# Sums of the upper tiles taken from turned blocks, eight transposes per tile, in the entries of a Strassen-like decoder block

## Chip, cores, metric

One Trainium2 core of one chip runs the whole kernel. The metric is the device time of one execution in microseconds (us). Before the change three runs gave 1890.28, 1890.79 and 1891.32 us; the median is 1890.79.

## The reference

The kernel computes one decoder block in fp32: two SwiGLU half-steps around a gated mixer. All of it is matrix products over 1024 rows of 1024 numbers, with a norm of the rows ahead of each part.

```python
def swiglu(x, w1, w3, w2):
    return (jax.nn.silu(x @ w1) * (x @ w3)) @ w2
...
        h = h + 0.5 * swiglu(rms_norm(h, ffn1_norm[l]), ffn1_w1[l], ffn1_w3[l], ffn1_w2[l])
...
    return rms_norm(h, final_norm)
```

Between the first half-step and a second one of the same form stands the mixer: its input is rms(h) times one combined weight (queries, keys, values, pooling, gates), and its output is added to h. What the change touches is how the left operand of three of these products, the normed rows X of the first half-step, of the mixer and of the second half-step, is turned and summed.

## The kernel before

**Sevens.** Each of these products is done in quarters: X is turned and cut into four blocks of 512 by 512, b11 and b21 from the first four tiles of 128 rows (their columns 0 to 511, `LOWS`, and 512 to 1023, `HIGHS`), b12 and b22 likewise from the last four. A product of 2 by 2 blocks takes seven block products in place of eight. `Quad.run` names them by number: 1 takes b11, 2 takes b21, 3 takes b22, 4 takes the sum t4, 5 takes t1, 6 takes t2 and 7 takes t3. Here t1 = b12 - b11, t2 = b22 - t1, t3 = b22 - b12 = t2 - b11 and t4 = t2 - b21. The turned b11 and b21 are kept in SBUF as `low`. The weights have sums of their own: s1 (L370), s2 (L374), s3 (L378), s4 (L383), made in `Quad.summed`.

**Two parts.** Every fp32 operand is split in a rounded part (hi, written by ScalarE) and a lower part (lo = value - hi, by VectorE or GpSimd). For weights that is `Sevens.split` (L320 ScalarE, L323 VectorE or GpSimd), for X it is `Rows` (transposes L409, hi L411, lo L416) and `Parts` (hi L429, lo L432). A product is three groups of four matmuls (L332): hi by hi, lo by hi, hi by lo.

**Entries.** `Entry.run` treats tiles 4 to 7 (the upper tiles). It runs three times: in the first half-step (some 36 to 65 us in the profile), in the mixer (654 to 682) and in the second half-step (1249 to 1278). For each tile it does two products whose operands are ready (`self.product(i)`, `self.product(k)`: numbers 1 and 2 on several column blocks of weights), and between them the next tile's rows are normed (`high(t, 1)`, the row scaling of L282 on VectorE, whose 1/rms is a power on GpSimd, L279) and turned. `self.operand(n)` makes the two parts of the weight for a later product on ScalarE and GpSimd, `self.out(n)` takes a finished product's bank on, `self.more(...)` makes operands of the first products behind the entry: `more(0, 2)` makes s2 on GpSimd, `more(0)` splits it for product 6, `more(1)` makes and splits s3 for product 7. Behind the last tile come products 6, 7, 5 and 4 (t2, t3, t1, t4).

**What sets the order.** Each engine executes its instructions in the order in which the code writes them (a manual schedule); semaphores make one engine wait for another. A wait at the head of an engine's list holds all behind it. The banks of PSUM named "acc" and "mm" are given out in turn.

Before, a tile has 12 transposes: 4 of b22 (`Rows`), 4 of b12 (`turned`, L477) and 4 of the row difference (`HIGHS` less `LOWS`) that GpSimd makes ahead of them (L461) and that gives t3 turned. VectorE makes t1 in place in the bank of b12 (L471), t2 by adding b11 to the turned t3 (L465), t4 in place of t2 (L468), and all the lower parts of X.

Of the kernel before, what the change touches and what calls it, by code (L numbers as in the profile page):

```python
# [10 lines left out]
F32 = mybir.dt.float32  # L11
F32R = mybir.dt.float32r
AF = mybir.ActivationFunctionType
OP = mybir.AluOpType
# [5 lines left out]
NT = S // P  # L20
# [117 lines left out]
def tile_block(  # L138
# [29 lines left out]
    ve, ac, gp, pe = nc.vector, nc.scalar, nc.gpsimd, nc.tensor  # L168
# [10 lines left out]
    def bank(tag, name):  # L179
        return psum.tile([P, HALF], F32, tag=tag, name=name)  # L180
# [18 lines left out]
    h = []  # L199
# [98 lines left out]
    LOWS, HIGHS = slice(0, HALF), slice(HALF, S)  # L298
# [7 lines left out]
    class Sevens:  # L306


        def __init__(self, name, X, fw, fs=None):
            self.name, self.X, self.fw, self.fs = name, X, fw, fs or fw  # L310
            self.n_lo = 0
            self.terms = (0, 1, 2)
            self.led = {}
# [86 lines left out]
    class Rows:  # L400
# [14 lines left out]
        def lower(self):  # L415
            ve.tensor_tensor(self.lo, self.p, self.hi.bitcast(F32), op=OP.subtract)  # L416
# [5 lines left out]
    class Parts:  # L422


        def __init__(self, X, what, src, t):
            q = t % 4
            self.hi, self.lo = (v[:, :, q * P:(q + 1) * P] for v in X[what])
            self.src = src.rearrange("p (k q) -> p k q", k=4)
            ac.activation(self.hi, self.src, AF.Copy)  # L429

        def lower(self):
            ve.tensor_tensor(self.lo, self.src, self.hi.bitcast(F32), op=OP.subtract)  # L432

    class Entry:

# [17 lines left out]
        def run(self, high, after, first=0):  # L453


            X = self.sv.X

            def scaled_rows(t):
                y = high(t, 1)
                t3 = self.sv.half_tile("s", f"t3_{t}")  # L460
                gp.tensor_tensor(t3, y[:, HIGHS], y[:, LOWS], op=OP.subtract)  # L461
                return y, t3

            def second(r3, t2, t):
                ve.tensor_tensor(t2, r3.flat, self.low[t - 4][:, LOWS], op=OP.add)  # L465

            def fourth(t2, t):
                ve.tensor_tensor(t2, t2, self.low[t - 4][:, HIGHS], op=OP.subtract)  # L468

            def first_less(p12, t):  # L470
                ve.tensor_tensor(p12, p12, self.low[t - 4][:, LOWS], op=OP.subtract)  # L471

            def turned(y, t):
                p12 = bank("acc", f"x_b12_{t}")
                for j in range(4):
                    c = slice(j * P, (j + 1) * P)
                    pe.transpose(p12[:, c], y[:, c], ident)  # L477
                return p12

            y, t3 = scaled_rows(4)  # L480
            for t in range(4, NT - 1):
                i = first + 2 * (t - 4)
                k = i + 1
                self.product(i)
                self.operand(i + 2)
                high(t + 1, 0)
                s = Rows(X, "b22", y[:, HIGHS], t)
                self.out(i)
                p12 = turned(y, t)
                first_less(p12, t)  # L490
                r1 = Parts(X, "t1", p12, t)
                r3 = Rows(X, "t3", t3, t)
                t2 = bank("acc", f"x_t2_{t}")
                s.lower()
                r1.lower()
                self.product(k)
                y, t3 = scaled_rows(t + 1)
                self.operand(k + 2)
                second(r3, t2, t)
                r2 = Parts(X, "t2", t2, t)  # L500
                r3.lower()
                r2.lower()
                self.out(k)
                after(t)
                fourth(t2, t)
                if t < NT - 2:
                    r4 = Parts(X, "t4", t2, t)
                    if t > 4:
                        self.more(0, 1)
                    r4.lower()  # L510

            t = NT - 1
            i, k = i + 2, k + 2
            self.product(i)
            p3 = bank("acc", f"x_t3_{t}")
            p12 = turned(y, t)
            s = Rows(X, "b22", y[:, HIGHS], t, "mm")
            r3 = Rows(X, "t3", t3, t, p=p3)
            r4 = Parts(X, "t4", t2, t - 1)
            self.more(0, 2)  # L520
            t2 = bank("acc", f"x_t2_{t}")
            second(r3, t2, t)
            r4.lower()
            r2 = Parts(X, "t2", t2, t)
            r3.lower()
            self.more(0)
            r2.lower()
            self.product(k)
            self.out(i)
            first_less(p12, t)  # L530
            r1 = Parts(X, "t1", p12, t)
            self.more(1)
            r1.lower()
            fourth(t2, t)
            r4 = Parts(X, "t4", t2, t)
            s.lower()
            r4.lower()
            self.out(k)
            after(t)


# [364 lines left out]
    X = sums_of_x(scope.enter_context(sbuf("x1")), "f1", SUMS)  # L906
# [1099 lines left out]
    first = first_w_o()  # L2006
    with tc.manual_schedule():
# [8 lines left out]
        for q in range(N // 2):  # L2016
# [20 lines left out]
            u, i = divmod(q, NT // 2)  # L2037
# [59 lines left out]
    op = wo.enter_context(sbuf("ops", "right"))  # L2097
# [390 lines left out]
```

## Time and profile before

| what | us |
|---|---|
| median of three runs | 1890.79 |
| span of the profiled execution | 1888.4 |
| TensorE busy (8806 matmuls) | 1878.1 |
| VectorE busy | 1345.8 |
| ScalarE busy | 773.1 |
| GpSimd busy | 715.0 |

The median stands 2.4 us above the span; the profiled execution's own time beyond its span is not known, and the 2.4 us are taken for what lies around it. TensorE is named PE, VectorE DVE, ScalarE ACT, GpSimd POOL. A row of the timeline gives the start from the span's beginning, the duration, the engine, the line, the operation, what is written and read, the count of like instructions in the row, and in brackets how long the engine had been idle and for what it waited. Names such as `x_t` and `x_b` are banks of PSUM (the turned sums and blocks of X), `xhi_t`, `xlo_t`, `xhi_b`, `xlo_b` the two parts of X's sums and blocks, `wc` the two parts of a weight, `s_` sums of weights or rows, `u_` the banks of the products, `nst` the norm's column. `f1`, `mix` and `f2` stand for the three entries.

### The profile page before, as it was taken

The numbers are of one execution on the slowest core, as the hardware profiler recorded it, in microseconds if no ns is written. First come the engines' busy times: TensorE is split into PE (matmuls) and PEld (weight loads), VectorE is DVE, ScalarE is ACT, GpSimd is POOL, SyncE is SP. The second block draws the span as 40 slices with busy tenths as digits, with TensorE's granted clock in tenths as the row PEclk, the third lists the DMA queues.
The fourth block names the chain that finished last, engine by engine and source line by source line (L and its number), as shares of the span: only waits on it lengthen the run. The fifth ranks groups of instructions, "written<-read, shape, count | busy, mean of one in ns | idle before, by whom it ended". The sixth has DMA issues, their size and how long they took to land.

```text
span 1888.4 us, 24712 instructions
## 1 busy us (share of the span) xinstructions
PE 1878.1 (99%) x8806; PEld 1559.8 (83%) x8806; DVE 1345.8 (71%) x1988; ACT 773.1 (41%) x1395; POOL 715.0 (38%) x536
## 2 busy tenths in 40 slices
PE   9999999999999999999999999999999999999998
PEld 8888888888888888888888888888888888888886
DVE  6877666558786776657885897887665566577867
ACT  7423333333344543334445772363233333334344
POOL 5433333331223354434555357543333333312221
PEclk9999999999999999999999999999999999999999
DMA  6154423336565526765578968644332223354654
GB/s 258 34 201 158 139 93 115 126 117 217 171 230 197 184 90 217 231 221 200 206 245 315 321 221 297 260 150 155 140 129 96 87 102 118 135 193 159 225 198 145
DMA packets 146035, 334.98 MB, mean 177 GB/s; under 512 B 17784, under 2 KB 39288, under 8 KB 144376
## 3 DMA queue, kind: packets, MB, share of 16 engines
q1 hardware_dynamic: 142168, 322.55, 49.4%
q10 hardware_dynamic: 3744, 10.85, 1.6%
q8 instruction: 69, 1.13, 0.2%
q14 instruction: 54, 0.44, 0.1%
HBM read 232.76 MB, written 100.60 MB: 177 GB/s over the span
## 4 chain that ended last, share of the span: by engine, by line
PE 54%; DVE 3%; ACT 2%; issue 1%; DMA 1%; POOL 0%; ACTq 0%; SPq 0%; DVEq 0%; POOLq 0%
PE u_mixm L332 15%; PE d_f L846 8%; PE wo L2168 4%; PE yp L1910 1%; PE u_f20b L332 1%; PE u_f21a L332 1%; PE u_f210b L332 1%; PE u_f210a L332 1%; PE u_f29b L332 1%; PE u_f29a L332 1%; PE u_f28b L332 1%; PE u_f28a L332 1%; PE u_f27b L332 1%; PE u_f27a L332 1%; PE u_f26b L332 1%; PE u_f25b L332 1%
## 5 line engine op out<-in xcount | busy, mean ns | idle before, releaser
L846 PE MATMUL d_f<-bhi_f,ahi_f 128*128 128x512 f32 x616 | 240.2, 390 | 0.0
L846 PE MATMUL d_f<-bhi_f,alo_f 128*128 128x512 f32 x616 | 239.7, 389 | 0.0
L846 PE MATMUL d_f<-blo_f,ahi_f 128*128 128x512 f32 x616 | 239.6, 389 | 0.0
L803 POOL TENSOR_TENSOR alo_f<-g_f,ahi_f 128x512 fp32r<-128x512 f32 x60 | 86.5, 1457 | 273.1 <-ACT ahi_f L799 273.1
L332 PE MATMUL u_mixm<-xhi_t_mix,wc_mixm 128*128 128x512 f32 x608 | 157.3, 391 | 0.2 <-ACT wc_mixm L320 0.2
L846 PEld LDWEIGHTS d_f<-bhi_f,ahi_f 128*128 128x128 f32 x616 | 115.6, 188 | 24.2 <-ACT h L420 0.4
L846 PEld LDWEIGHTS d_f<-bhi_f,alo_f 128*128 128x128 f32 x616 | 115.6, 188 | 24.1
L846 PEld LDWEIGHTS d_f<-blo_f,ahi_f 128*128 128x128 f32 x616 | 115.6, 188 | 23.9
L332 PEld LDWEIGHTS u_mixm<-xhi_t_mix,wc_mixm 128*128 128x128 f32 x608 | 113.5, 188 | 24.0 <-ACT wc_mixm L320 0.7
L332 PE MATMUL u_mixm<-xhi_b_mix,wc_mixm 128*128 128x512 f32 x456 | 120.3, 391 | 0.0
L323 POOL TENSOR_TENSOR wc_mixm<-s_mixm,wc_mixm 128x512 fp32r<-128x512 f32 x52 | 76.8, 1477 | 107.1 <-ACT wc_mixm L320 94.2
L332 PEld LDWEIGHTS u_mixm<-xhi_b_mix,wc_mixm 128*128 128x128 f32 x456 | 84.9, 188 | 17.3
L320 ACT ACTIVATE wc_mixm<-s_mixm 128x512 fp32r<-128x512 f32 x76 | 47.0, 628 | 111.8 <-DVE s_mixm L374 56.0
L799 ACT ACTIVATE ahi_f<-g_f 128x1024 fp32r<-128x1024 f32 x84 | 81.9, 975 | 4.9 <-DMA g_f<-gs_f 4.9
L332 PE MATMUL u_mixm<-xlo_t_mix,wc_mixm 128*128 128x512 f32 x304 | 81.3, 389 | 0.0
L323 POOL TENSOR_TENSOR wc_mixm<-raw,wc_mixm 128x512 fp32r<-128x512 f32 x40 | 60.2, 1505 | 40.2 <-ACT wc_mixm L320 29.5
L2168 PE MATMUL wo<-w_o,o_hi 128*128 128x512 f32 x224 | 69.4, 391 | 0.0
L799 ACT ACTIVATE bhi_f<-s_f2w 128x512 fp32r<-128x512 f32 x55 | 32.9, 628 | 86.3 <-DVE s_f2w L821 67.3
L799 ACT ACTIVATE bhi_f<-s_f1w 128x512 fp32r<-128x512 f32 x55 | 33.0, 629 | 83.6 <-DVE s_f1w L821 70.3
L332 PEld LDWEIGHTS u_mixm<-xlo_t_mix,wc_mixm 128*128 128x128 f32 x304 | 57.1, 188 | 12.0
L803 DVE TENSOR_TENSOR alo_f<-g_f,ahi_f 128x1024 fp32r<-128x1024 f32 (+1 forms) x48 | 57.6, 1200 | 9.4 <-ACT ahi_f L799 9.4
L332 PE MATMUL u_mixm<-xlo_b_mix,wc_mixm 128*128 128x512 f32 x228 | 61.0, 389 | 0.0
(1351 smaller groups left out, 4765.5 us busy)
## 6 DMA issues: line engine op xcount, KB each, us to landing
g_f<-gs_f SPq DMA_DIRECT2D x70, 512.0 KB
gs_f<-y_f SPq DMA_DIRECT2D x88, 256.0 KB
raw<-in_w2a_dram SPq DMA_DIRECT2D x35, 512.0 KB
raw<-in_w2b_dram SPq DMA_DIRECT2D x35, 512.0 KB
gs_f<-gb_f SPq DMA_DIRECT2D x46, 256.0 KB
raw<-in_w1a_dram SPq DMA_DIRECT2D x22, 512.0 KB
raw<-in_w3a_dram SPq DMA_DIRECT2D x22, 512.0 KB
raw<-in_w1b_dram SPq DMA_DIRECT2D x22, 512.0 KB
```

Source lines behind the costliest of these rows:

```text
L320: ac.activation(w[:, 0], src, AF.Copy)
L323: eng.tensor_tensor(w[:, 1], src, w[:, 0].bitcast(F32), op=OP.subtract)
L332: pe.matmul(p, a, b, start=(start and n == 0), stop=(n == 11), skip_group_check=not start)
L799: ac.activation(hi[:, c], src, AF.Copy)
L803: eng.tensor_tensor(lo[:, d], src[:, o], hi[:, d].bitcast(F32), op=OP.subtract)
L846: pe.matmul(self.banks[m][t], l, r, start=(first and q == 0), stop=(last and q == 2))
L1910: pe.matmul(p, a, b, start=(j == 0), stop=(j == 11))
L2168: pe.matmul(banks[m][t], l, r, start=(st == 0 and j == 0 and q == 0), stop=(st == 1 and j == 1 and q == 2))
```

## The change

Of each upper tile only b22 and b12 are turned: 8 transposes. The row difference on GpSimd and its 4 transposes go. t1 = b12 - b11 is written to the lower half of the tile's own rows in SBUF (`h[t][:, LOWS]`), t2 = b22 - t1 goes into a bank, t3 = t2 - b11 over the bank of b12, t4 = t2 - b21 to the upper half of the tile's own rows. `Parts` gets a `higher()` that may be issued later, and a `lower(eng)`. In tiles 4 to 6 the lower parts of t1 and t4 are made by GpSimd, t4's hi and lo one tile later. The operand of product i + 2 is now asked for ahead of its tile as `operand(i + 4)` at the end of the tile before. In tile 7 the order of sums, parts, `more` and `out` is another.

```diff
-        def __init__(self, X, what, src, t):
+        def __init__(self, X, what, src, t, now=True):
...
+            if now:
+                self.higher()
+
+        def higher(self):
             ac.activation(self.hi, self.src, AF.Copy)
 
-        def lower(self):
-            ve.tensor_tensor(self.lo, self.src, self.hi.bitcast(F32), op=OP.subtract)
+        def lower(self, eng=ve):
+            eng.tensor_tensor(self.lo, self.src, self.hi.bitcast(F32), op=OP.subtract)
...
             def scaled_rows(t):
-                y = high(t, 1)
-                t3 = self.sv.half_tile("s", f"t3_{t}")
-                gp.tensor_tensor(t3, y[:, HIGHS], y[:, LOWS], op=OP.subtract)
-                return y, t3
-
-            def second(r3, t2, t):
-                ve.tensor_tensor(t2, r3.flat, self.low[t - 4][:, LOWS], op=OP.add)
+                return high(t, 1)
+
+            def first_less(p12, t):
+                t1 = h[t][:, LOWS]
+                ve.tensor_tensor(t1, p12, self.low[t - 4][:, LOWS], op=OP.subtract)
+                return t1
+
+            def second(s, t1, t2):
+                ve.tensor_tensor(t2, s.flat, t1, op=OP.subtract)
+
+            def third(t2, p, t):
+                ve.tensor_tensor(p, t2, self.low[t - 4][:, LOWS], op=OP.subtract)
 
             def fourth(t2, t):
-                ve.tensor_tensor(t2, t2, self.low[t - 4][:, HIGHS], op=OP.subtract)
-
-            def first_less(p12, t):
-                ve.tensor_tensor(p12, p12, self.low[t - 4][:, LOWS], op=OP.subtract)
+                t4 = h[t][:, HIGHS]
+                ve.tensor_tensor(t4, t2, self.low[t - 4][:, HIGHS], op=OP.subtract)
+                return t4
...
+            def turned_rows(y, t, tag="acc"):
+                return Rows(X, "b22", y[:, HIGHS], t, tag)
+
+            y = scaled_rows(4)
+            self.operand(first + 2)
+            r4 = None
             for t in range(4, NT - 1):
                 i = first + 2 * (t - 4)
                 k = i + 1
                 self.product(i)
-                self.operand(i + 2)
                 high(t + 1, 0)
-                s = Rows(X, "b22", y[:, HIGHS], t)
+                s = turned_rows(y, t)
+                p12 = turned(y, t)
                 self.out(i)
-                p12 = turned(y, t)
-                first_less(p12, t)
-                r1 = Parts(X, "t1", p12, t)
-                r3 = Rows(X, "t3", t3, t)
+                if r4 is not None:
+                    r4.higher()
+                    r4.lower(gp)
+                t1 = first_less(p12, t)
                 t2 = bank("acc", f"x_t2_{t}")
                 s.lower()
-                r1.lower()
+                second(s, t1, t2)
                 self.product(k)
-                y, t3 = scaled_rows(t + 1)
+                y = scaled_rows(t + 1)
+                r2 = Parts(X, "t2", t2, t)
+                r1 = Parts(X, "t1", t1, t)
+                third(t2, p12, t)
+                r1.lower(gp)
                 self.operand(k + 2)
-                second(r3, t2, t)
-                r2 = Parts(X, "t2", t2, t)
-                r3.lower()
                 r2.lower()
                 self.out(k)
+                r3 = Parts(X, "t3", p12, t)
+                r3.lower()
+                r4 = Parts(X, "t4", fourth(t2, t), t, False)
                 after(t)
-                fourth(t2, t)
-                if t < NT - 2:
-                    r4 = Parts(X, "t4", t2, t)
-                    if t > 4:
-                        self.more(0, 1)
-                    r4.lower()
+                self.operand(i + 4)
+                if t > 4:
+                    self.more(0, 1)
 
             t = NT - 1
             i, k = i + 2, k + 2
             self.product(i)
-            p3 = bank("acc", f"x_t3_{t}")
             p12 = turned(y, t)
-            s = Rows(X, "b22", y[:, HIGHS], t, "mm")
-            r3 = Rows(X, "t3", t3, t, p=p3)
-            r4 = Parts(X, "t4", t2, t - 1)
+            s = turned_rows(y, t, "mm")
+            r4.higher()
+            r4.lower(gp)
+            t1 = first_less(p12, t)
+            t2 = bank("acc", f"x_t2_{t}")
+            second(s, t1, t2)
             self.more(0, 2)
-            t2 = bank("acc", f"x_t2_{t}")
-            second(r3, t2, t)
-            r4.lower()
             r2 = Parts(X, "t2", t2, t)
+            third(t2, p12, t)
+            self.more(0)
+            self.out(i)
+            r2.lower()
+            r3 = Parts(X, "t3", p12, t)
             r3.lower()
-            self.more(0)
-            r2.lower()
             self.product(k)
-            self.out(i)
-            first_less(p12, t)
-            r1 = Parts(X, "t1", p12, t)
+            r1 = Parts(X, "t1", t1, t)
+            r4 = Parts(X, "t4", fourth(t2, t), t, False)
             self.more(1)
             r1.lower()
-            fourth(t2, t)
-            r4 = Parts(X, "t4", t2, t)
+            r4.higher()
+            self.out(k)
             s.lower()
             r4.lower()
-            self.out(k)
             after(t)
```

What this does to the order on the engines is shown at the end of the mixer's entry. First GpSimd, from the weights of tile 6 to the first products behind the entry; `s_mixt` are the row differences, `xlo_t_mix<-h` lower parts of t1 and t4, L374 is s2. Before:

```order
L323 TENSOR_TENSOR wc_mixm_5662<-raw_5398,wc_mixm_5662 128x512
L323 TENSOR_TENSOR wc_mixm_5688<-raw_5336,wc_mixm_5688 128x512
L279 TENSOR_TENSOR nst_5602<-nst_5602,mhalf 128x1
L461 TENSOR_TENSOR s_mixt_7_5731<-hn_mix_5601 128x512
L323 TENSOR_TENSOR wc_mixm_5733<-raw_5398,wc_mixm_5733 128x512
L374 TENSOR_TENSOR s_mixm_5773<-s_mixm_5672,raw_5287 128x512
L323 TENSOR_TENSOR wc_mixm_5780<-s_mixm_5773,wc_mixm_5780 128x512
```

The same stretch of GpSimd after the change:

```order
L323 TENSOR_TENSOR wc_mixm_5625<-raw_5374,wc_mixm_5625 128x512
L323 TENSOR_TENSOR wc_mixm_5633<-raw_5312,wc_mixm_5633 128x512
L279 TENSOR_TENSOR nst_5571<-nst_5571,mhalf 128x1
L436 TENSOR_TENSOR xlo_t_mix<-h_3181,xhi_t_mix 128x4x128
L436 TENSOR_TENSOR xlo_t_mix<-h_3183,xhi_t_mix 128x4x128
L323 TENSOR_TENSOR wc_mixm_5690<-raw_5374,wc_mixm_5690 128x512
L436 TENSOR_TENSOR xlo_t_mix<-h_3183,xhi_t_mix 128x4x128
L374 TENSOR_TENSOR s_mixm_5727<-s_mixm_5636,raw_5263 128x512
L323 TENSOR_TENSOR wc_mixm_5731<-s_mixm_5727,wc_mixm_5731 128x512
```

The row difference is gone, two lower parts stand in its place, and a third (t4 of tile 6) stands ahead of s2.

Next ScalarE in tile 7 of the mixer's entry, from the rounding of b22 on; `xhi_t_mix<-x_t_7` and `x_b_7` are roundings of the sums in banks, `wc_mixm<-s_mixm` those of s2 and s3, `y_m` output copies. Before:

```order
L411 ACTIVATE xhi_b_mix<-x_b_7_5761 128x4x128
L411 ACTIVATE xhi_t_mix<-x_t_7_5755 128x4x128
L429 ACTIVATE xhi_t_mix<-x_t_6_5714 128x4x128
L429 ACTIVATE xhi_t_mix<-x_t_7_5775 128x4x128
L320 ACTIVATE wc_mixm_5780<-s_mixm_5773 128x512
L1233 ACTIVATE y_m_0_5699<-u_mixm_5675 128x512
L429 ACTIVATE xhi_t_mix<-x_b_7_5756 128x4x128
L320 ACTIVATE wc_mixm_5801<-s_mixm_5799 128x512
```

The same stretch of ScalarE after the change (`h_3183` holds t1 and t4 of tile 6, `h_3185` those of tile 7):

```order
L411 ACTIVATE xhi_b_mix<-x_b_7_5716 128x4x128
L433 ACTIVATE xhi_t_mix<-h_3183 128x4x128
L433 ACTIVATE xhi_t_mix<-x_t_7_5725 128x4x128
L320 ACTIVATE wc_mixm_5731<-s_mixm_5727 128x512
L1247 ACTIVATE y_m_0_5664<-u_mixm_5638 128x512
L433 ACTIVATE xhi_t_mix<-x_b_7_5711 128x4x128
L433 ACTIVATE xhi_t_mix<-h_3185 128x4x128
L320 ACTIVATE wc_mixm_5754<-s_mixm_5752 128x512
```

The rounding of t3, second in the list before, now stands behind the rounding of s2 and an output copy; t4 of tile 6 stands directly behind b22.

Last VectorE in the same tile, from the sums to s3 (L378). Before:

```order
L465 TENSOR_TENSOR x_t_7_5775<-x_t_7_5755,h_3201 128x512
L432 TENSOR_TENSOR xlo_t_mix<-x_t_6_5714,xhi_t_mix 128x4x128
L416 TENSOR_TENSOR xlo_t_mix<-x_t_7_5755,xhi_t_mix 128x4x128
L432 TENSOR_TENSOR xlo_t_mix<-x_t_7_5775,xhi_t_mix 128x4x128
L471 TENSOR_TENSOR x_b_7_5756<-x_b_7_5756,h_3201 128x512
L378 TENSOR_TENSOR s_mixm_5799<-raw_5287,raw_5401 128x512
```

The same stretch of VectorE after the change:

```order
L467 TENSOR_TENSOR h_3185<-x_b_7_5711,h_3177 128x512
L471 TENSOR_TENSOR x_t_7_5725<-x_b_7_5716,h_3185 128x512
L474 TENSOR_TENSOR x_b_7_5711<-x_t_7_5725,h_3177 128x512
L436 TENSOR_TENSOR xlo_t_mix<-x_t_7_5725,xhi_t_mix 128x4x128
L436 TENSOR_TENSOR xlo_t_mix<-x_b_7_5711,xhi_t_mix 128x4x128
L478 TENSOR_TENSOR h_3185<-x_t_7_5725,h_3177 128x512
L378 TENSOR_TENSOR s_mixm_5752<-raw_5263,raw_5377 128x512
```

The lower part of t3 (the second L436), which waits for t3's rounding on ScalarE, and the fourth sum (L478) now stand ahead of s3.

More of the change, by code (lines that the diff above doesn't have):

```diff
@@ L478, in turned @@
                 return p12
-            y, t3 = scaled_rows(4)
+            def turned_rows(y, t, tag="acc"):
[3 more added lines that the diff above has]
+            r4 = None
             for t in range(4, NT - 1):
```

## The prediction

> **What bounds the kernel now.** First the busy shares on the page, then the waits of TensorE alone.
>
> ```profile
> span 1888.4 us, 24712 instructions
> PE 1878.1 (99%) x8806; PEld 1559.8 (83%) x8806; DVE 1345.8 (71%) x1988; ACT 773.1 (41%) x1395; POOL 715.0 (38%) x536
> PEclk9999999999999999999999999999999999999999
> ```
>
> ```profile
> PE idle L967 <- DVE mhalf L198: 1.1, 1, 1.1
> PE x_t L409 <- POOL s_f1t L461: 0.8, 1, 0.8
> PE o L1851 <- DVE elo L1833: 0.3, 1, 0.3
> ```
>
> TensorE works for 1878.1 of 1888.4 us at full granted clock, and its longest wait inside the work is 0.8 us, once, on the difference that GpSimd makes for the first entry. So time goes away only where TensorE gets less to do or that wait goes, and any new wait of TensorE is added to the span: nothing later has slack to take it back. The run's own time is the span plus 2.4 us (1890.79 against 1888.4); a measurement of this kernel tells about 0.2% (3.8 us) from no change.
>
> **What goes.** One whole upper tile of the mixer's entry on TensorE, then the first of the first entry:
>
> ```profile
> 661.05 0.60 PE L409 MATMUL x_b<-ident,hn_mix 128*128 128x128 f32 x4
> 661.49 0.60 PE L477 MATMUL x_b<-ident,hn_mix 128*128 128x128 f32 x4
> 661.92 0.60 PE L409 MATMUL x_t<-ident,s_mixt 128*128 128x128 f32 x4
> 662.28 1.17 PE L332 MATMUL u_mixm<-xhi_b_mix,wc_mixm 128*128 128x512 f32 x4
> ```
>
> ```profile
> 36.83 0.60 PE L477 MATMUL x_b<-ident,x 128*128 128x128 f32 x4
> 38.25 0.65 PE L409 MATMUL x_t<-ident,s_f1t 128*128 128x128 f32 x4 [0.82 <-POOL s_f1t L461]
> ```
>
> Groups of four transposes start 0.44 us apart, although each group's bar is 0.60 us long (they overlap); three groups take 662.28 - 661.05 = 1.23 us. I take 0.435 us for the group that goes. Four tiles in three entries give 12 x 0.435 = 5.2 us, and the 0.82 us wait goes with its writer: 6.0 us in all. The Trainium skill, "TensorE: Matmul & The Clock Gate", Part 4, gives about 275 ns for a transpose in one kernel's context; by that 48 of them would be worth an estimated 13.2 us. The rows disagree: the pitch decides, 0.109 us each.
>
> **What is late next.** In each entry the path leaves the transposes at the last tile (7), where the first products on the new sums begin. The rows of the mixer's entry, engine by engine; t2 names the product at 678.76, t3 the next, which starts 0.91 us into the 680.71 row (half of it), at 681.62.
>
> ```profile
> 674.66 0.60 PE L477 MATMUL x_b<-ident,hn_mix 128*128 128x128 f32 x4
> 675.10 0.60 PE L409 MATMUL x_b<-ident,hn_mix 128*128 128x128 f32 x4
> 678.76 1.19 PE L332 MATMUL u_mixm<-xhi_t_mix,wc_mixm 128*128 128x512 f32 x4
> 680.71 2.00 PE L332 MATMUL u_mixm<-xhi_t_mix,wc_mixm 128*128 128x512 f32 x8
> ```
>
> ```profile
> 674.46 1.27 POOL L323 TENSOR_TENSOR wc_mixm<-raw,wc_mixm 128x512 fp32r<-128x512 f32 x1
> 675.70 1.28 POOL L374 TENSOR_TENSOR s_mixm<-s_mixm,raw 128x512 f32<-128x512 f32 x1
> 678.79 1.30 POOL L323 TENSOR_TENSOR wc_mixm<-s_mixm,wc_mixm 128x512 fp32r<-128x512 f32 x1 [1.81 <-ACT wc_mixm L320]
> ```
>
> ```profile
> 675.74 0.60 ACT L411 ACTIVATE xhi_b_mix<-x_b 128x512 fp32r<-128x512 f32 x1 [0.89 <-PE x_b L409]
> 676.23 0.59 ACT L411 ACTIVATE xhi_t_mix<-x_t 128x512 fp32r<-128x512 f32 x1
> 678.09 0.62 ACT L320 ACTIVATE wc_mixm<-s_mixm 128x512 fp32r<-128x512 f32 x1
> 678.61 0.59 ACT L1233 ACTIVATE y_m<-u_mixm 128x512 f32<-128x512 f32 x1
> 679.98 0.60 ACT L429 ACTIVATE xhi_t_mix<-x_b 128x512 fp32r<-128x512 f32 x1 [0.79 <-DVE x_b L471]
> 680.73 0.63 ACT L320 ACTIVATE wc_mixm<-s_mixm 128x512 fp32r<-128x512 f32 x1
> ```
>
> ```profile
> 679.26 0.69 DVE L471 TENSOR_TENSOR x_b<-x_b,h 128x512 f32<-128x512 f32 x1
> 679.86 0.78 DVE L378 TENSOR_TENSOR s_mixm<-raw,raw 128x512 f32<-128x512 f32 x1
> 680.62 0.69 DVE L432 TENSOR_TENSOR xlo_t_mix<-x_b,xhi_t_mix 128x512 fp32r<-128x512 f32 x1
> ```
>
> TensorE is fed just in time already: weight sum s2 (L374) leaves GpSimd at 676.98, its rounded part (L320) starts at 678.09, t2 at 678.76, 0.67 us behind. Before, s2 stands right behind a weight's lower part (674.46). After, the order puts the lower part of tile 6's t4 between them, and that waits for its rounded part on ScalarE, behind the rounding of tile 7's b22, which waits for tile 7's transposes. So s2 hangs on the transposes, in a chain that TensorE cannot run ahead of.
>
> Working it out. Three groups fewer bring tile 7's first transposes to 674.66 - 1.31 = 673.35. Steps from the rows: second group +0.44; its rounding +0.64 (675.10 to 675.74), at 674.43; t4's rounding +0.49, at 674.92; GpSimd +0.70 (678.09 to 678.79), at 675.62; s2 +1.24 (674.46 to 675.70), at 676.86; its rounding +1.37 (s2's 1.28 and a hop of 0.09, as from 679.86 + 0.78 to 680.73), at 678.23; t2 +0.67, at **678.90**: nothing of the 1.74 us that four groups saved is left (678.76).
>
> t3 is later still. ScalarE has t3's rounding behind s2's rounding and an output copy: 678.23 + 0.52 + 0.49 = 679.24. VectorE's lower part of t3 waits for it (+0.64, 679.98 to 680.62), at 679.88, and the fourth sum and s3 (L378) stand behind that wait: s3 at 679.88 + 0.60 + 0.60 = 681.08. Its rounding +0.87, at 681.95; t3's product +0.67, at **682.62** against 681.62: **+1.0 us**, where t2's end would have allowed 681.76. In the chain's own terms t3 starts 9.27 us behind tile 7's first transposes. In the other two entries the same last tile stands:
>
> ```profile
> 57.83 0.60 PE L477 MATMUL x_b<-ident,x 128*128 128x128 f32 x4
> 63.88 1.98 PE L332 MATMUL u_f10a<-xhi_t_f,wc_f10a 128*128 128x512 f32 x8
> 1269.93 0.60 PE L477 MATMUL x_b<-ident,hn_f 128*128 128x128 f32 x4
> 1276.40 2.07 PE L332 MATMUL u_f20a<-xhi_t_f,wc_f20a 128*128 128x512 f32 x8
> ```
>
> First entry: 57.83 - 1.31 - 0.82 + 9.27 = 64.97 against 64.79, +0.2. Third: 1269.93 - 1.31 + 9.27 = 1277.89 against 1277.31, +0.6. Chain alone: **+1.8 us** for the three, the 6.0 us already spent in it.
>
> **VectorE against GpSimd.** What the two do at once:
>
> ```profile
> 33.06 2.31 DVE L282 SCALAR_TENSOR_TENSOR x<-x,nst,gain_ffn 128x1024 f32<-128x1024 f32 x1
> 664.57 1.27 DVE L282 SCALAR_TENSOR_TENSOR hn_mix<-h,nst,gain_mix 128x1024 f32<-128x1024 f32 x1
> 1244.95 1.27 DVE L282 SCALAR_TENSOR_TENSOR hn_f<-h_again,nst,gain_ffn 128x1024 f32<-128x1024 f32 x1
> ```
>
> ```profile
> 32.91 1.37 POOL L323 TENSOR_TENSOR wc_f10a<-raw,wc_f10a 128x512 fp32r<-128x512 f32 x1
> 663.82 0.55 POOL L279 TENSOR_TENSOR nst<-nst,mhalf 128x1 f32<-128x1 f32 x1
> 1245.18 1.45 POOL L279 TENSOR_TENSOR nst<-nst,mhalf 128x1 f32<-128x1 f32 x1 [1.00 <-DVE nst L278]
> ```
>
> The row scaling takes 1.27 us with GpSimd idle, 2.31 when GpSimd began 0.15 us earlier (+1.04); and GpSimd's power of 0.55 takes 1.45 when the scaling began first. One works, the other stands. The Trainium skill, "SBUF — State Buffer", Who interferes with whom, speaks against the change here: a VectorE instruction with two SBUF inputs and a GpSimd one that reads SBUF contend for a shared port, and the first holds it for its whole instruction. Its rule agrees with the rows; by it each new overlap could cost up to a whole GpSimd instruction, an estimated 1.29 us.
>
> GpSimd had per tile two weight lower parts, a power and a difference: 2 x 1.25 + 0.55 + 1.25 = 4.3 us of a tile's 6.8. It loses the difference and gains two lower parts: 5.55 of 6.4 (6.8 less 0.44), with the scaling (1.28) falling into the same tile: together 6.8, so tiles 5 to 7 must overlap. VectorE's other work there has a PSUM operand and seems spared (679.26 took 0.69 us inside GpSimd's 678.79 to 680.09), but tile 7's two lower parts now read SBUF alone. Bounds per entry on the path: nothing, or two overlaps of 1.04. I take one: **3 x 1.04 = 3.1 us**.
>
> **GpSimd's lower part** (128x4x128, strided out) has no row before. Below: 1.25 us as counted. Above:
>
> ```profile
> L323 POOL TENSOR_TENSOR wc_mixm<-raw,wc_mixm 128x512 fp32r<-128x512 f32 x40 | 60.2, 1505 | 40.2 <-ACT wc_mixm L320 29.5
> ```
>
> 1.505, a mean with overlaps in it. With GpSimd full, six of them an entry would add 18 x 0.25 = 4.5 us. I take 1.25, nearest to the rows without overlap.
>
> **The rest at nothing.** Sums written to the rows' own tiles: same instruction, same engine. VectorE loses six instructions and waits for TensorE anyway. Operands two ahead are now asked for at a tile's end, so a 512 KB weight load starts later; SP's own order stays. Between 36 and 50 us, in slices of 0.35 us:
>
> ```profile
> DMA  0000000009399810002000000009699800000000
> ```
>
> Two such loads fill six slices each at most, 2.1 us, against a tile of 6.8 us; wholly uncovered, one would cost 2.1 us, and I keep that in the heavy case below.
>
> **Sum.** +1.8 + 3.1 = +4.9 us: a span of 1893.3, **1895.7 us**, 0.26% slower.
>
> **Rivals.** *Gain kept* (0.12): the chain is not waited for and 6.0 us stay, 1884.8. For it: TensorE's 99% and a kernel that waits nearly nowhere. Against: t2 in the mixer's entry would have to start at 677.02, so s2 on GpSimd at 677.02 - 0.67 - 1.37 = 674.98, 0.06 us after t4's rounding can even begin on ScalarE. It needs s2 ahead of that lower part; the order has it behind. *Chain alone* (0.33): overlaps fall beside the path, +1.8, 1892.6: no difference that can be told. *GpSimd becomes the bound* (0.15): its lower parts take 1.5 us, 4.5 more, 1900.2, with a late weight load 1902.3; it decides once GpSimd's 5.55 us plus overlaps pass a tile's 6.4.
>
> **How the numbers follow.** Forecast 0.40, the rivals as given. Faster by over 0.2%: 0.12. Within: the chain alone and a tenth of the forecast (its edge is 1894.6), 0.37. Slower: 0.51. The range leaves out most of the first rival and half of the last: 1887.5 to 1900.5. The likeliest case's own: 1892.6 to 1898.8 (none to two overlaps an entry, +1.8 to +8.0).
>
> **What would show it.** Right: four transpose groups of 0.44 us gone per entry; TensorE waiting at t2 or t3 in each entry on ScalarE's roundings of s2 and s3; s2 on GpSimd directly behind tile 6's lower part, some 3.5 us behind tile 7's first transposes (676.86 - 673.35); scalings of over 2 us, or lower parts on GpSimd of 2 us and more, in tiles 5 to 7. Wrong: no such wait (then the gain stands); waits before products inside tiles 4 to 6 (then GpSimd bounds the entry, or a load is late); lower parts of 1.5 us with VectorE elsewhere.

## The result and the profile after

The changed kernel takes 1895.45 us (median of ten runs, 1894.32 to 1896.61), the kernel before 1890.38 us beside it: a ratio of 1.0025, 95% interval 1.0016 to 1.0034. It is slower by 5.1 us, or 0.25%; 1895.7 us were forecast. Its busy shares on the page, and then the waits of TensorE (in all, times, longest):

```profile
span 1893.5 us, 24607 instructions
PE 1875.3 (99%) x8758; PEld 1556.0 (82%) x8758; DVE 1346.6 (71%) x1982; ACT 774.1 (41%) x1395; POOL 726.2 (38%) x542
```

```profile
PE u_mixm L332 <- ACT wc_mixm L320: 3.1, 2, 2.6
PE u_f20a L332 <- ACT wc_f20a L320: 2.7, 2, 2.3
PE u_f10a L332 <- ACT wc_f10a L320: 2.5, 1, 2.5
```

TensorE has 48 instructions fewer and works 2.8 us less, and the wait of 0.8 us on the row difference is gone. In its place stand three groups of waits, 8.3 us together, all on ScalarE's rounding of weights and weight sums (L320). Of the mixer's 3.1 us, 0.53 stand at 741.96 us, long behind its entry, where the kernel before waits 0.16; directly behind the three entries stand 2.53, 2.57 and 2.29 + 0.40 us, 7.8 us in all. The page's shares say nothing of it: 99% before and after.

Where the 5.1 us come in is read from the first transposes of each entry, of the kernel before and of the changed one:

```profile
36.39 0.60 PE L409 MATMUL x_b<-ident,x 128*128 128x128 f32 x4
654.26 0.60 PE L409 MATMUL x_b<-ident,hn_mix 128*128 128x128 f32 x4
1249.53 0.60 PE L409 MATMUL x_b<-ident,hn_f 128*128 128x128 f32 x4
```

```profile
36.05 0.60 PE L409 MATMUL x_b<-ident,x 128*128 128x128 f32 x4
655.35 0.60 PE L409 MATMUL x_b<-ident,hn_mix 128*128 128x128 f32 x4
1253.06 0.60 PE L409 MATMUL x_b<-ident,hn_f 128*128 128x128 f32 x4
```

The distance to the next entry, or to the span's end, grew by 1.43, 2.44 and 1.57 us (the first entry began 0.34 us earlier). Each stretch has one entry in it, and the list of waits has nothing new that is longer than 0.4 us but the three groups above.

The last tile of the mixer's entry, engine by engine, in the changed kernel (start, duration, engine, line; in brackets the idle time ahead and what ended it). TensorE:

```profile
674.41 0.60 PE L485 MATMUL x_b<-ident,hn_mix 128*128 128x128 f32 x4
680.75 2.08 PE L332 MATMUL u_mixm<-xhi_t_mix,wc_mixm 128*128 128x512 f32 x4 [2.57 <-ACT wc_mixm L320]
682.63 1.61 PE L332 MATMUL u_mixm<-xlo_t_mix,wc_mixm 128*128 128x512 f32 x4
```

ScalarE and GpSimd at the same place:

```profile
676.82 0.63 ACT L433 ACTIVATE xhi_t_mix<-h 128x512 fp32r<-128x512 f32 x1 [0.74 <-DVE h L478]
...
680.07 0.63 ACT L320 ACTIVATE wc_mixm<-s_mixm 128x512 fp32r<-128x512 f32 x1 [1.25 <-POOL s_mixm L374]
683.68 0.63 ACT L320 ACTIVATE wc_mixm<-s_mixm 128x512 fp32r<-128x512 f32 x1 [1.49 <-DVE s_mixm L378]
```

```profile
677.53 1.28 POOL L436 TENSOR_TENSOR xlo_t_mix<-h,xhi_t_mix 128x512 fp32r<-128x512 f32 x1 [0.93 <-ACT xhi_t_mix L433]
678.77 1.27 POOL L374 TENSOR_TENSOR s_mixm<-s_mixm,raw 128x512 f32<-128x512 f32 x1
```

The chain stands there link by link: the rounding of tile 6's t4 (676.82), its lower part on GpSimd (677.53), s2 directly behind (678.77), s2's rounding (680.07), t2's product (680.75, 0.68 behind). Only its first link differs from the forecast: t4's rounding waits for the fourth sum on VectorE (L478), not for ScalarE's rounding of b22. VectorE is late, and two tiles earlier one sees why:

```profile
664.59 2.17 DVE L282 SCALAR_TENSOR_TENSOR hn_mix<-h,nst,gain_mix 128x1024 f32<-128x1024 f32 x1
669.24 1.72 DVE L370 TENSOR_TENSOR s_mixm<-raw 128x512 f32<-128x512 f32 x1
676.11 0.68 DVE L478 TENSOR_TENSOR h<-x_t,h 128x512 f32<-128x512 f32 x1
```

```profile
664.38 1.29 POOL L436 TENSOR_TENSOR xlo_t_mix<-h,xhi_t_mix 128x512 fp32r<-128x512 f32 x1
665.91 2.00 POOL L436 TENSOR_TENSOR xlo_t_mix<-h,xhi_t_mix 128x512 fp32r<-128x512 f32 x1 [0.24 <-ACT xhi_t_mix L433]
```

The scaling takes 2.17 us where GpSimd's new lower part began 0.21 us earlier, and the next lower part takes 2.00 where the scaling was under way. So VectorE comes to the weight sum s1 (L370) later, which then runs beside two lower parts of weights on GpSimd (667.88 to 670.41) and takes 1.72 us for 0.68 before.

One thing had no place in the forecast. Behind the long wait the four matmuls at 680.75 take 1.88 us up to the next group, against 1.03 before. The granted clock in stretches of that time (us of the stretch, TensorE busy, clock, DMA share, GB/s) shows the reason:

```profile
677.00:680.40 3.40, 1.18 (x6) 0.99 0.26 75
680.40:683.80 3.40, 3.05 (x7) 0.50 0.17 58
```

For some 3.4 us TensorE has half its clock, and 1.00 again in the next 3.4; the same happens behind the first entry (62.4 to 65.8 us), not behind the third, where the wait was 2.29 us. The rows add up: 7.8 us of waits, and 3.0 us by which the matmuls behind the first two entries take longer than before (1.6 and 1.4), less the 6.0 us set free, are 4.8 of the 5.1 us.

### The profile page after: what moved, and what is told of

The parts are those of the page before. It is cut to its first block, busy times and chain, and to the rows that moved or that the text cites. A ratio compares the mean times of both kernels' runs of the same rounds, so it can differ in the third digit from the quotient of the medians.

```text
span 1893.5 us, 24607 instructions
## 1 busy us (share of the span) xinstructions
PE 1875.3 (99%) x8758; PEld 1556.0 (82%) x8758; DVE 1346.6 (71%) x1982; ACT 774.1 (41%) x1395; POOL 726.2 (38%) x542
## 5 line engine op out<-in xcount | busy, mean ns | idle before, releaser
L320 ACT ACTIVATE wc_mixm<-s_mixm 128x512 fp32r<-128x512 f32 x76 | 47.0, 628 | 113.2 <-DVE s_mixm L374 54.7
```

The costliest lines, as they stand in the source:

```text
L320: ac.activation(w[:, 0], src, AF.Copy)
```

## Experiments

Lines of code are those of the changed kernel unless said otherwise. Beside each group of runs the kernel before took 1890.4 to 1890.7 us.

### One part of the change alone

In the kernel before, tile 6's t4 goes to its own rows and its lower part is made by GpSimd ahead of s2. All 12 transposes per tile stay.

```diff
+                if t == NT - 2:
+                    t4 = h[t][:, HIGHS]
+                    ve.tensor_tensor(t4, t2, self.low[t - 4][:, HIGHS], op=OP.subtract)
...
-            r4 = Parts(X, "t4", t2, t - 1)
+            r4 = Parts(X, "t4", t4, t - 1)
+            r4.lower(gp)
             self.more(0, 2)
             t2 = bank("acc", f"x_t2_{t}")
             second(r3, t2, t)
-            r4.lower()
```

> The kernel before, with its 12 transposes per tile, and one part of the change alone: tile 6's t4 is written to the tile's own rows and its lower part made by GpSimd ahead of s2. Chain theory: s2 starts behind t4's rounding (mixer 676.71) + 0.70 + 1.25 = 678.66 in place of 675.70, its rounding at 680.03, t2's product at 680.70 in place of 678.76: 1.94 us per entry, 5.8 us in all, about 1896.2 us; the wait is under 2 us, so the clock stays. Rival (the position of that lower part is not what counts): 1890.4.

Measured: 1895.94 us, ratio 1.0030 (1.0019 to 1.0041). GpSimd and TensorE in the mixer's entry of this run:

```profile
678.92 1.29 POOL L432 TENSOR_TENSOR xlo_t_mix<-h,xhi_t_mix 128x512 fp32r<-128x512 f32 x1 [1.67 <-ACT xhi_t_mix L429]
680.17 1.27 POOL L374 TENSOR_TENSOR s_mixm<-s_mixm,raw 128x512 f32<-128x512 f32 x1
682.16 1.20 PE L332 MATMUL u_mixm<-xhi_t_mix,wc_mixm 128*128 128x512 f32 x4 [1.76 <-ACT wc_mixm L320]
```

One lower part ahead of s2 costs 5.5 us in three entries, 1.8 us each: the kernel before had no slack at this place. The rival falls.

### The same part undone in the changed kernel

```diff
             r4.higher()
+            self.more(0, 2)
             r4.lower(gp)
             t1 = first_less(p12, t)
             t2 = bank("acc", f"x_t2_{t}")
             second(s, t1, t2)
-            self.more(0, 2)
```

> Changed kernel, but in tile 7 the weight sum s2 is issued on GpSimd ahead of tile 6's last lower part. Chain theory: s2 no longer hangs on tile 7's transposes; its rounding then stands right behind t2's rounding on ScalarE (mixer: 678.22 + 0.49 = 678.7 in place of 680.07), t2's product starts 1.4 us earlier in each entry, the wait of TensorE falls from 2.3-2.6 to about 1.2 us, and with it the half clock that followed the longer waits goes (0.6 us more in the first two entries): about 1890.1 us, level with before. Rival (GpSimd and VectorE standing in each other's way is the whole loss): no instruction less on either, so about 1895.4.

Measured: 1889.82 us, ratio 0.9997 (0.9988 to 1.0006), 5.6 us less than the changed kernel. One call moved up by four lines takes the whole loss away; the stretches at half clock go with it. TensorE still waits at t2 and t3, as forecast for this run:

```profile
677.51 1.19 PE L332 MATMUL u_mixm<-xhi_t_mix,wc_mixm 128*128 128x512 f32 x4 [1.22 <-ACT wc_mixm L320]
681.12 1.19 PE L332 MATMUL u_mixm<-xhi_t_mix,wc_mixm 128*128 128x512 f32 x4 [0.59 <-ACT wc_mixm L320]
```

The matmuls behind these shorter waits take 1.19 us: the clock stayed.

### Work that nobody reads, in the wait

```diff
             self.product(k)
+            idle = bank("acc", "x_idle")
+            for n in range(16):
+                c = slice(n % 4 * P, (n % 4 + 1) * P)
+                pe.transpose(idle[:, c], ident, ident)
             r1 = Parts(X, "t1", t1, t)
```

> Changed kernel with 16 more transposes of the identity into an unused bank between the last ready product and t2's product, 1.74 us of TensorE work that nobody reads, in the stretch where it waits. Clock theory: TensorE's idle time falls from 2.5 to 0.8 us, the granted clock stays at 1.00 behind it (0.50 for 3 us in the changed kernel's first and second entry), t3's product starts 0.6 us earlier in these two: about 1894.2 us. Rival (the slow stretch is the wait for lower parts): the same clock or the same time, 1895.4. If the fill were on the path: 1897 or more.

Measured: 1894.27 us, ratio 1.0021 (1.0011 to 1.0030). The fill, t2's product behind it, and the clock from there to t3's product:

```profile
677.37 1.91 PE L548 MATMUL x_idle<-ident 128*128 128x128 f32 x16
680.12 1.19 PE L332 MATMUL u_mixm<-xhi_t_mix,wc_mixm 128*128 128x512 f32 x4 [0.84 <-ACT wc_mixm L320]
```

```profile
680.10:683.70 3.60, 3.02 (x12) 1.00 0.06 20
```

With the idle time cut from 2.57 to 0.84 us the half clock does not come in any entry, and 1.2 us go, as expected (between medians; the ten runs, 1893.8 to 1896.0 us, overlap those of the changed kernel). It cost less than its 3.4 us at half speed, because the wait for s3 would have held t3 in any case: it is seen in this run as 0.60 us of idle time.

### Lower parts set to zero

```diff
-                    r4.lower(gp)
+                    gp.memset(r4.lo.bitcast(F32), 0.0)
...
-                r1.lower(gp)
+                gp.memset(r1.lo.bitcast(F32), 0.0)
```

> Changed kernel, but GpSimd's lower parts of t1 (tiles 4 to 6) and of t4 (tiles 4 and 5) are set to zero there instead of being subtracted: these 15 lower parts are left out, at the same place in GpSimd's order, by an instruction that reads no SBUF. Tile 6's t4, ahead of s2, stays. Overlap theory (VectorE with two SBUF inputs stands against GpSimd's reading): the scaling of tile 6 goes from 2.17 back to 1.27 us and s1 from 1.72 to 0.7-1.3, VectorE is 0.8 us less late in tile 7, t2's product starts 0.8 us earlier in each entry, TensorE's wait falls to 1.8 us and the half clock goes: about 1891.7 us. Rival (VectorE is late for its ten instructions a tile alone, or for ScalarE): the wait stays at 2.3 to 2.6 us, 1895.4.

Measured: 1892.09 us, ratio 1.0008 (0.9999 to 1.0017), 3.4 us less than the changed kernel. VectorE and GpSimd at the place where the scaling took 2.17 us, and TensorE at t2:

```profile
663.18 1.28 DVE L282 SCALAR_TENSOR_TENSOR hn_mix<-h,nst,gain_mix 128x1024 f32<-128x1024 f32 x1
```

```profile
662.94 0.53 POOL L504 MEMSET xlo_t_mix<- 128x512 f32 x1
663.40 0.53 POOL L514 MEMSET xlo_t_mix<- 128x512 f32 x1
```

```profile
678.51 1.20 PE L332 MATMUL u_mixm<-xhi_t_mix,wc_mixm 128*128 128x512 f32 x4 [1.73 <-ACT wc_mixm L320]
```

The scaling runs beside two instructions of GpSimd that write SBUF without reading it, and none of the three is stretched; beside a subtraction it took 2.17 us. The Trainium skill, "SBUF — State Buffer", Who interferes with whom, says just this of GpSimd instructions that only write; the rows agree. VectorE is in time for tile 7, and the wait falls from 2.57 to 1.73 us. Here the forecast chain stands as it was worked out, its first link too, to 0.06 us at every link. ScalarE rounds tile 7's b22 at 674.07 us and t4 right behind it at 674.57; the first transposes of tile 7, then the lower part and s2 on GpSimd:

```profile
673.00 0.60 PE L485 MATMUL x_b<-ident,hn_mix 128*128 128x128 f32 x4
```

```profile
675.27 1.29 POOL L436 TENSOR_TENSOR xlo_t_mix<-h,xhi_t_mix 128x512 fp32r<-128x512 f32 x1 [2.01 <-ACT xhi_t_mix L433]
676.52 1.27 POOL L374 TENSOR_TENSOR s_mixm<-s_mixm,raw 128x512 f32<-128x512 f32 x1
```

t2's product starts 5.51 us behind these transposes (5.51 and 5.50 in the other entries), 5.55 were forecast; in the changed kernel it is 6.34. The clock stays behind the first two entries; behind the third it is 0.50 from 1276.3 to 1279.7 us in the profiled execution (1892.94 us, one of the slower ones of this kernel), although the wait there was only 1.70 us. So the expectation that the half clock goes held in part. What is left against the kernel before, 1.4 us, is the chain without overlaps, forecast as 1.8; the median may hold some half clock still. The run gives GpSimd less to do as well (0.53 us for 1.29); what of the 3.4 us is due to that was not separated.

### t1's lower part back on VectorE

```diff
-                r1.lower(gp)
+                r1.lower()
```

> Changed kernel, but the lower part of t1 in tiles 4 to 6 is made by VectorE again (nine instructions moved off GpSimd). Overlap theory: GpSimd has 4.3 us of work per tile, the stretched row scaling (2.17 us) and s1 (1.72 us) go back to 1.27 and 0.7-0.8, VectorE is no longer 0.8 us late in tile 7, and TensorE's wait falls by 0.8 us per entry, with the half clock behind it gone: about 1891.7 us. Rival (only the order of s2 and s3 costs): the chain from tile 7's transposes to s2 is as long as it was, about 1895.4. Second rival: VectorE with three more instructions of 0.6 us per entry becomes late itself: 1896 or more.

Measured: 1897.86 us, ratio 1.0038 (1.0024 to 1.0052), 2.4 us more than the changed kernel: the second rival. The scaling of tile 6 and the waits in this run:

```profile
666.10 2.16 DVE L282 SCALAR_TENSOR_TENSOR hn_mix<-h,nst,gain_mix 128x1024 f32<-128x1024 f32 x1
```

```profile
PE u_mixm L332 <- ACT wc_mixm L320: 2.9, 2, 2.7
PE u_f20a L332 <- ACT wc_f20a L320: 2.9, 1, 2.9
PE u_f10a L332 <- ACT wc_f10a L320: 2.9, 1, 2.9
```

It was the wrong lower part to move: the scaling meets t4's, which stayed. And in the tile that also makes s1 VectorE has nine instructions of 0.60 us and a scaling (9 x 0.60 + 1.2 = 6.6 us of a tile's 6.36), so it falls behind even without overlaps; which of the two costs how much was not separated. Now the third entry's wait is 2.9 us too, and the half clock follows there as well (1281.4 to 1284.7 us).

### s2 ahead, and s3 ahead of t3

```diff
             second(s, t1, t2)
-            self.more(0, 2)
+            self.more(1, 1)
```

s2 stands where the run with s2 ahead has it; `more(1, 1)` sums s3 alone.

> The run with s2 ahead (1889.8), and besides s3 summed on VectorE before it waits for t3's rounding. Theory: t3's product no longer waits (0.55, 0.59 and 0.41 us in that run), t2's stays as it was: about 1888.3 us. Rival (t3 waits for ScalarE's own order, its rounding, not for s3): 1889.8.

Measured: 1890.51 us, ratio 1.0002 (0.9992 to 1.0011), a miss by 2.2 us. t3 waits no longer, as the theory had it, but s3, which reads two SBUF operands, now runs beside a lower part of GpSimd (676.02, 1.27 us):

```profile
676.31 1.53 DVE L378 TENSOR_TENSOR s_mixm<-raw,raw 128x512 f32<-128x512 f32 x1
```

```profile
679.09 1.65 PE L332 MATMUL u_mixm<-xlo_t_mix,wc_mixm 128*128 128x512 f32 x4 [0.29 <-DVE xlo_t_mix L436]
```

```profile
676.20:679.60 3.40, 1.89 (x7) 1.00 0.25 88
679.60:683.00 3.40, 3.40 (x9) 0.50 0.06 23
```

It takes 1.53 us for 0.68, t2's lower part behind it is late, and TensorE waits for that. In the profiled execution the half clock came too, behind 1.89 us of work in 3.4. The ten runs spread, five from 1889.2 to 1889.9 and five from 1891.1 to 1893.0 us, so this is not the same every time; even the first five are above the 1888.3 expected.

### The order around tile 7 written anew

```diff
+                if t == NT - 2:
+                    self.more(0, 1)
                 third(t2, p12, t)
-                r1.lower(gp)
+                if t < NT - 2:
+                    r1.lower(gp)
...
-                r3.lower()
-                r4 = Parts(X, "t4", fourth(t2, t), t, False)
+                if t < NT - 2:
+                    r3.lower()
+                    r4 = Parts(X, "t4", fourth(t2, t), t, False)
+                else:
+                    self.more(0, 2)
+                    r1.lower(gp)
...
-                if t > 4:
-                    self.more(0, 1)
...
             s = turned_rows(y, t, "mm")
-            r4.higher()
-            r4.lower(gp)
             t1 = first_less(p12, t)
-            t2 = bank("acc", f"x_t2_{t}")
+            r3.lower()
+            t26, t2 = t2, bank("acc", f"x_t2_{t}")
             second(s, t1, t2)
-            self.more(0, 2)
+            self.more(0)
             r2 = Parts(X, "t2", t2, t)
-            third(t2, p12, t)
-            self.more(0)
-            self.out(i)
+            r4 = Parts(X, "t4", fourth(t26, t - 1), t - 1, False)
+            self.more(1, 1)
             r2.lower()
+            third(t2, p12, t)
+            self.out(i)
+            r4.higher()
+            r4.lower(gp)
             r3 = Parts(X, "t3", p12, t)
+            self.more(1)
             r3.lower()
...
-            self.more(1)
```

> Changed kernel with another order around tile 7: s2 ahead of tile 6's lower parts on GpSimd and rounded ahead of t2 on ScalarE, s3 before t3 is waited for, tile 6's t3 and t4 behind tile 7's first sum on VectorE, s1 behind the scaling of tile 7. The same instructions. Theory (only the waits at t2 and t3 eat the gain): waits of TensorE behind the three entries fall from 8.3 us to under 1.5, the 5 to 6 us of the transposes and of the first wait show: about 1885.5 us. Rival (something else holds what the transposes set free): not under 1889.

Measured: 1886.93 us, ratio 0.9981 (0.9971 to 0.9991). It was measured once more beside a later run:

> The reordered run again, on the chip of the run beside it: 1886.9 us, 0.2% under the kernel before, if its gain is no accident of one chip.

1886.52 us, ratio 0.9978 (0.9969 to 0.9987). This beats both kernels, by 4 us the one before and by 9 the changed one, with the changed kernel's own instructions. The waits of TensorE that are left behind the entries (of the repeat):

```profile
PE u_f10a L332 <- ACT xhi_t_f L433: 0.9, 1, 0.9
PE u_f20a L332 <- DVE xlo_t_f L436: 0.5, 1, 0.5
PE u_mixm L332 <- ACT xhi_t_mix L433: 0.5, 1, 0.5
PE u_mixm L332 <- DVE xlo_t_mix L436: 0.2, 1, 0.2
PE u_f10a L332 <- DVE xlo_t_f L436: 0.2, 1, 0.2
```

They are 2.3 us in place of 7.8, not under 1.5 as expected, and of the 6.0 us set free some 4 show: the gain was there, and the order ate it.

### Three tries at the overlaps that are left

In the reordered run scalings of 2.2 us remain. First, t4's lower parts later on GpSimd, behind the next weight's (and in tile 6 behind s2):

```diff
                     r4.higher()
-                    r4.lower(gp)
...
                 self.operand(k + 2)
+                if r4 is not None and t < NT - 2:
+                    r4.lower(gp)
...
                     self.more(0, 2)
-                    r1.lower(gp)
+                    r4.lower(gp)
...
             self.more(0)
+            r1.lower(gp)
```

> The reordered run (1886.9), and besides t4's lower parts on GpSimd are issued behind the next weight's lower part, so that the row scaling on VectorE starts while GpSimd has nothing to read. The same instructions. Overlap theory: the scaling of tiles 6 and 7 (2.19 and 2.18 us) goes back to 1.27, VectorE is in time for tile 7, and TensorE's remaining waits of 0.5 to 1.0 us per entry go: about 1885.0 us. Rival (GpSimd's amount of work is what makes VectorE late, wherever it stands): other VectorE rows stretch in its place, 1886.9.

Measured: 1888.69 us, ratio 0.9991 (0.9981 to 1.0000): 1.8 us more, not less. The scalings did go back to 1.27 and 1.28 us, so the overlap theory holds for them (s3 on VectorE is stretched in their place, from 0.91 to 1.39 us in the mixer's entry), but a new wait stands in the first entry, on ScalarE and then on TensorE:

```profile
57.77 0.60 ACT L634 ACTIVATE u<-u_f12b 128x512 f32<-128x512 f32 x1 [4.35 <-POOL xlo_t_f L436]
```

```profile
58.42 1.20 PE L332 MATMUL u_f12b<-xhi_b_f,wc_f12b 128*128 128x512 f32 x4 [2.24 <-ACT u L634]
```

The output copy (L634) takes a buffer of rows that GpSimd's late lower part still reads; until that is done, the product's bank isn't free. Second, only tile 4's lower part later, so that no rows are held:

```diff
                     r4.higher()
-                    r4.lower(gp)
+                    if t == NT - 2:
+                        r4.lower(gp)
...
                 self.operand(k + 2)
+                if r4 is not None and t < NT - 2:
+                    r4.lower(gp)
```

> The reordered run, with tile 4's lower part of t4 alone issued later on GpSimd (in tile 5 behind the next weight's lower part, in tile 6 where the reordered run has it). Overlap theory: the scaling of tile 6 goes from 2.19 to 1.27 us, that of tile 7 stays at 2.2, nobody waits for rows that t4 holds; VectorE is up to 0.9 us earlier in tile 7 and TensorE's waits of 0.5 to 1.1 us per entry halve: about 1885.7 us. Rival (VectorE catches up before tile 7 either way): 1886.9.

Measured: 1888.73 us, ratio 0.9992 (0.9983 to 1.0000), 2.2 us above the reordered run beside it. The scaling of tile 6 is 1.28 us again, but VectorE gains nothing: it waits 0.49 us for the power on GpSimd, and the scaling of tile 7 takes 2.30 us. TensorE's waits behind the entries grow from 2.3 to 3.9 us. Third, the power behind t4's lower part:

```diff
-                high(t + 1, 0)
                 s = turned_rows(y, t)
...
                     r4.lower(gp)
+                high(t + 1, 0)
                 t1 = first_less(p12, t)
```

> The reordered run (1886.9), and besides the power of the next tile's norm is issued on GpSimd behind t4's lower part, so that the scaling, which waits for it, starts when that lower part is done, and t4's lower part is not late for whoever takes its rows (as it was in the run with lower parts later). The same instructions. Overlap theory: scalings of 2.2 us go back to 1.27 where the power stands in the entry (tiles 6 and 7 of the first two entries, tile 7 of the third), TensorE's remaining waits of 0.5 to 1.1 us per entry shrink by about half: 1885.5 us. Rival (the scaling comes as late behind the power as it ended in the overlap): 1886.9.

Measured: 1891.22 us, ratio 1.0004 (0.9995 to 1.0013), a clear miss, and worse than the rival: the scaling now waits 1.27 us for the power and then meets the next lower part.

```profile
665.70 2.33 DVE L282 SCALAR_TENSOR_TENSOR hn_mix<-h,nst,gain_mix 128x1024 f32<-128x1024 f32 x1 [1.27 <-POOL nst L279]
```

With GpSimd as full as this, an overlap taken out at one place came back at another in all three.

### The price of the transposes alone

The run with t4's lower parts later, and four more transposes of the identity per tile.

```diff
+            def again(t):
+                p = bank("acc", f"x_again_{t}")
+                for j in range(4):
+                    pe.transpose(p[:, j * P:(j + 1) * P], ident, ident)
...
                 p12 = turned(y, t)
+                again(t)
...
             s = turned_rows(y, t, "mm")
+            again(t)
```

> The run with t4's lower parts later, and besides four more transposes of the identity per upper tile into a bank that nobody reads: as many transposes as the kernel before has. Price of the transposes measured alone: 12 groups of 0.435 us, 5.2 us more than the run beside it. Rival (transposes run beside other work of TensorE): less than 2 us more; rival at the other end (each costs its 0.27 us): 13 us more.

Measured: 1890.98 us, 2.3 us more than the run beside it. Busy shares of that run and of this one:

```profile
PE 1872.5 (99%) x8758; PEld 1554.3 (82%) x8758; DVE 1346.0 (71%) x1982; ACT 773.4 (41%) x1395; POOL 724.7 (38%) x542
```

```profile
PE 1877.9 (99%) x8806; PEld 1560.3 (83%) x8806; DVE 1345.6 (71%) x1982; ACT 773.7 (41%) x1395; POOL 722.2 (38%) x542
```

TensorE's work grows by 5.4 us, so the price of 5.2 is right as work; as time it is missed. Only half of it reaches the span (1886.0 to 1888.8 us), because the run beside it had waits which the transposes filled: its longest, 2.24 us, is 0.90 here.

## Why the prediction was right, and where it was not

**What goes** (6.0 us): right in mechanism and size. TensorE's tile went from 6.80 to 6.36 us, the first entry's wait is gone, and the last experiment prices the transposes at 5.4 us of TensorE's work. The estimate by the figure of the Trainium skill, "TensorE: Matmul & The Clock Gate", Part 4 (about 275 ns a transpose, 13.2 us), does not come out here.

**What is late next**: right. s2 behind the chain from tile 7's transposes and t4's rounding is shown from both sides: put into the kernel before it costs 5.5 us, taken out of the changed one it gives back 5.6 (some 1.2 of it the half clock, by the run with the fill). The chain's own size, forecast as 1.8 us above the kernel before, is 1.4 where the overlaps are taken away, and there its links stand where the forecast has them. In the changed kernel itself the first link was another: t4's rounding waited for VectorE, not for tile 7's transposes, and t2 stands 0.79 us later in the chain for it. t3's second delay shows in the changed kernel as 0.40 us of idle time behind the third entry alone; behind the other two the stretch at half clock hides it, and where the fill kept the clock it is 0.52 and 0.60 us, against 0.86 forecast for the mixer (682.62 - 681.76).

**VectorE against GpSimd**: right in mechanism, too big in size. One overlap of 1.04 us per entry was taken, 3.1 us. The rows show two stretched VectorE instructions in the mixer's entry (0.90 and 1.04 us more; the second, s1, beside lower parts of weights, which the forecast did not name) and two in each of the others (0.73 and 0.95, 0.63 and 0.62 us), of which slack took up a part: t2's wait fell by 0.84 us in the mixer's entry, by 0.80 in the first and 0.59 in the third when the lower parts no longer read, 2.2 us in all.

**Half clock**: missing in the forecast. It cost 1.2 us, by the run that took it away. Chain, overlaps and clock as measured (1.4, 2.2 and 1.2) give 4.8 of the 5.1 us, with perhaps some half clock in the 1.4 as well. So the sum of 4.9 us came out so close by luck, because the mis-sized overlap (3.1 for some 2.2) and the missing clock (1.2) nearly cancel. The term that the forecast lacked is this one: it let TensorE's waits cost only their own length.

**GpSimd's lower part**: 1.28 to 1.30 us where VectorE is elsewhere; the heavy case, in which it took 1.5, falls. **The rest at nothing**: no wait on a weight load stands in the changed kernel's list of TensorE's waits behind the entries.

**Signs**: s2 directly behind tile 6's lower part came, but 4.36 us behind tile 7's first transposes (678.77 - 674.41), not 3.5, as VectorE's lateness stood ahead of it (without the overlaps it is 676.52 - 673.00 = 3.52); no wait stood inside tiles 4 to 6.

What stays open: how much of the overlaps' cost is the port and how much GpSimd's fuller schedule; and what halves the clock: the length of the wait alone does not decide it.

## What to carry to other kernels

Before taking work off an engine that is always busy, look at what feeds it at the end of the stretch: here one weight sum arrived just in time, and its place in another engine's list was worth as much as the 48 transposes removed. Work moved to an idle engine is not free when it stands ahead of something on the path, or reads while another engine's two-operand instruction reads; count both. And before giving up on a change whose gain is missing, try its instructions in another order: the same ones gave 9 us less.

## What was not expected of the hardware

Waits of 2.5 to 2.9 us were followed by some 3.4 us at a granted clock of 0.50. Shorter ones went both ways: one of 1.70 us was followed by it, and so were 1.22 and 0.29 us within 3.4 us in one run; waits of 2.29, 2.24 and 1.77 us, and several of 1.2, were not. Filling the wait with transposes kept the clock at 1.00. Runs of the changed kernel with a mean clock of 0.997 or 0.998 took 1894.6 to 1896.6 us, the one with 0.999 took 1894.3. The Trainium skill, "TensorE: Matmul & The Clock Gate", Part 1, has a free-running window of 3413 ns, which the length here agrees with; its practical rule in the same part (HAM oscillation), no idle gap over some 3.4 us, is too wide for this case, where gaps of 1.70 to 2.90 us lost the clock.

GpSimd's setting to zero (0.53 us for 128x512) beside a two-operand scaling on VectorE stretched neither, while a subtraction beside it cost 0.9 us.
